# FFN gate and up products as seven-product units, with gated rows kept in DRAM

## The chip, the cores and the metric

The kernel runs on one core of a Trainium2 chip. The metric is the device time of one execution in microseconds. Five engines work beside each other, each in its own order: PE (TensorE, with weight loads as PEld), DVE (VectorE), ACT (ScalarE), POOL (GpSimd) and SP (SyncE), which here issues the DMA transfers.

## The reference

One layer of a decoder for 1024 prompt tokens and 8 sample tokens, 1032 columns together, width 1024, in fp32:

```python
# z = x @ w_in, one projection for all branches and gates
# A: conv4 -> RG-LRU times a gelu gate;  B: sliding-window attention;  C: attention into 256 memory tokens
# mix = (sum of branch @ w_branch, each times sigmoid(gate)) @ w_out
# x <- LN(alpha * x + mix)
# x <- LN(alpha * x + (silu(x @ w_gate) * (x @ w_up)) @ w_down)      D_FF = 2816 = 22 x 128
```

alpha is 2 ** 0.25. The caches of the window, with their new rows, are outputs too.

## The kernel before, in words

Every fp32 operand of a product is a pair, high part and rest (`split`, L69: a cast on ACT, a subtraction on DVE), and a product takes three matmuls (`mm3`, L105 to L107). Tokens lie in the columns: 1032 of them, cut in three chunks of 384, 384 and 264 (`CH`), or in quarters of 258 (`QN`).

Stage 1 (`project`) computes z in 30 units of two row blocks of w_in. A unit is a 2 x 2 block product by seven products instead of eight: both the weights and x enter as sums of their halves. The weight sums are made per unit (`fast_quarter`, L263, then split), three products ahead; a product is two quarters of 258 columns, 12 matmuls each (L279 to L281), 168 matmuls a unit. The sums of x are made once, in `begin`, beside unit 0 (which is computed directly, names u, th, thw) and unit 1. The names there: x and tl are a quarter of x and its rest, ur a raw weight half, us a weight sum, u_3h and u_3l the split of the weights of product 3, za and zb the results. A unit's results are finished by `Finish` (L369, L1182 to L1190).

The branches, the output projection and LN1 (`out_proj`, `layer_norm`) follow. LN1's last step `emit` splits h (hH, L1052, and hL, L1053) and has POOL scale the residual by alpha (L1054).

In the FFN (`ffn`) each of 22 f tiles takes 8 x 3 matmuls per chunk for the gate (fg) and as many for the up product (fu); ft holds silu times up (tanh on ACT, L1068; DVE, L1069 and L1071), and gH, gL its split. Eight, seven and seven f tiles make a part. Behind each of the first two stand its down products (d), added to the residual on DVE (L1095); behind the third those of the last part (dl) with LN2. Two copies of caches to outputs (o_swk, o_swv, 1 MB each) are issued behind the weight loads of f = 2 and f = 4.

The order on each engine is set by a list scheduler from the program's text and its estimates of when operands are ready; `issue_after` holds an instruction behind a given one. Weights pass through rings of six raw buffers of 512 columns, five for high parts and four for rests.

## Time and profile before

| quantity | value |
|---|---|
| median of 3 runs | 2013.3 us (2012.09 to 2013.93) |
| profiled run | 2013.24 us |
| its span, first to last instruction | 2011.5 us |
| mean granted TensorE clock | 0.994 |
| matmuls | 13756 |
| DVE, ACT instructions | 2558, 1921 |
| start of the FFN's first matmul | 1241.61 us |

Busy lines give an engine's busy time, its share of the span and the count of its instructions. In the windows view a row has the stretch, its length, then PE, weight loads, DVE, ACT and POOL as busy us with the count, then the granted clock, the DMA share and GB/s. A timeline row has start, duration, engine, line, operation and tiles, and in brackets the idle time before it with what released it. A group row has its count behind an x, then busy time, mean ns of one, and the idle time before. A DMA row ends with KB of each and the us from issue to landing.

### The profile page before, as it was taken

To read this page: it belongs to the slowest core of one execution; us is meant where nothing else is said; L and a number is where in the kernel's file an instruction comes from. 1 tells how busy PE (TensorE), PEld (TensorE's weight loads), DVE (VectorE), ACT (ScalarE), POOL (GpSimd) and SP (SyncE) were. 2 spreads that over 40 slices of the span, in tenths; PEclk is the share of its full clock that TensorE was granted. 3 is DMA by queue.
4 is the path that set the end of the run, shared out by engine and by line. 5 is a ranking of instruction groups with operands and counts; after the bars stand their busy time and mean duration, and the time that the engine had idled before them with its cause. 6 is when DMAs were issued, how large, how long until landed. Compare 5 with 4: busy or idle time off the path is not lost.

```text
span 2011.5 us, 35413 instructions
## 1 busy us (share of the span) xinstructions
PE 1962.2 (98%) x13756; PEld 1929.8 (96%) x13756; DVE 1197.3 (60%) x2558; ACT 878.9 (44%) x1921; POOL 112.4 (6%) x160
## 2 busy tenths in 40 slices
PE   7999999999999999999999999999999999999997
PEld 7999999999999899989999999999999999999996
DVE  8789778878665555498876658423222332232457
ACT  6556555546564555398763334322111221122324
POOL 0001000000000000021110002100000000000001
PEclk9999999999999999999999999999999999999999
DMA  5454454563233865667435320111111111111102
GB/s 220 151 174 171 165 190 137 176 197 125 76 142 107 294 217 188 160 187 218 121 87 167 124 87 22 63 63 58 48 43 42 53 49 47 53 43 43 57 28 85
DMA packets 140441, 235.44 MB, mean 117 GB/s; under 512 B 17280, under 2 KB 69584, under 8 KB 140240
## 3 DMA queue, kind: packets, MB, share of 16 engines
q1 hardware_dynamic: 140272, 233.17, 35.8%
q8 instruction: 108, 1.77, 0.4%
q14 instruction: 61, 0.50, 0.1%
HBM read 179.95 MB, written 55.23 MB: 117 GB/s over the span
## 4 chain that ended last, share of the span: by engine, by line
PE 70%; ACT 4%; DVE 3%; DMA 3%; issue 1%; SPq 0%; ACTq 0%; POOL 0%; DVEq 0%; POOLq 0%
PE fg L107 4%; PE fg L105 4%; PE fg L106 4%; PE fu L107 4%; PE fu L105 4%; PE fu L106 4%; PE d L105 3%; PE d L107 3%; PE d L106 3%; PE ub L279 2%; PE ub L281 2%; PE ub L280 2%; PE brs L105 2%; PE brs L106 2%; PE brs L107 1%; PE bra L106 1%
## 5 line engine op out<-in xcount | busy, mean ns | idle before, releaser
L105 PE MATMUL fg<-hH,wfg_h 128*128 128x384 f32 (+1 forms) x528 | 169.2, 320 | 5.9 <-ACT wfg_h L71 3.0
L106 PE MATMUL fg<-hL,wfg_h 128*128 128x384 f32 (+1 forms) x528 | 168.4, 319 | 0.4 <-DVE hL L1053 0.4
L107 PE MATMUL fg<-hH,wfg_l 128*128 128x384 f32 (+1 forms) x528 | 168.3, 319 | 0.2
L107 PE MATMUL fu<-hH,wfu_l 128*128 128x384 f32 (+1 forms) x528 | 167.7, 318 | 0.0
L106 PE MATMUL fu<-hL,wfu_h 128*128 128x384 f32 (+1 forms) x528 | 167.6, 317 | 0.0
L105 PE MATMUL fu<-hH,wfu_h 128*128 128x384 f32 (+1 forms) x528 | 167.6, 318 | 0.0
L1071 DVE TENSOR_TENSOR ft<-ft,fu 128x384 f32<-128x384 f32 (+1 forms) x66 | 33.8, 513 | 141.4 <-PE fu L107 141.3
L1069 DVE SCALAR_TENSOR_TENSOR ft<-ft,fg 128x384 f32<-128x384 f32 (+1 forms) x66 | 33.8, 512 | 139.6 <-ACT ft L1068 137.6
L105 PE MATMUL d<-gH,wd_h 128*128 128x384 f32 (+1 forms) x360 | 114.4, 318 | 0.0
L106 PE MATMUL d<-gL,wd_h 128*128 128x384 f32 (+1 forms) x360 | 114.2, 317 | 0.0
L107 PE MATMUL d<-gH,wd_l 128*128 128x384 f32 (+1 forms) x360 | 114.2, 317 | 0.0
L71 ACT CAST gH<-ft 128x384 fp32r<-128x384 f32 (+1 forms) x66 | 31.7, 480 | 183.2 <-DVE ft L1071 183.1
L105 PEld LDWEIGHTS fg<-hH,wfg_h 128*128 128x128 f32 x528 | 99.6, 189 | 7.3 <-ACT wfg_h L71 3.4
L106 PEld LDWEIGHTS fg<-hL,wfg_h 128*128 128x128 f32 x528 | 99.8, 189 | 1.0 <-DVE hL L1053 0.9
L107 PEld LDWEIGHTS fg<-hH,wfg_l 128*128 128x128 f32 x528 | 99.8, 189 | 0.9 <-DVE wfg_l L72 0.9
L107 PEld LDWEIGHTS fu<-hH,wfu_l 128*128 128x128 f32 x528 | 99.2, 188 | 0.0
L105 PEld LDWEIGHTS fu<-hH,wfu_h 128*128 128x128 f32 x528 | 99.2, 188 | 0.0
L106 PEld LDWEIGHTS fu<-hL,wfu_h 128*128 128x128 f32 x528 | 99.2, 188 | 0.0
L1068 ACT ACTIVATE ft<-fg 128x384 f32<-128x384 f32 (+1 forms) x66 | 30.1, 456 | 139.8 <-PE fg L107 139.8
L1095 DVE SCALAR_TENSOR_TENSOR acc<-d,acc 128x384 f32<-128x384 f32 (+1 forms) x48 | 24.8, 516 | 108.4 <-PE d L107 108.4
L565 ACT ACTIVATE bp<-bp,bst 128x257 f32<-128x257 f32 (+1 forms) x128 | 62.8, 493 | 18.1 <-DVE bst L561 18.0
L281 PE MATMUL uc<-th,u_3l 128*128 128x258 f32 x232 | 66.4, 287 | 4.1 <-DVE u_3l L72 4.1
(960 smaller groups left out, 6857.3 us busy)
## 6 DMA issues: line engine op xcount, KB each, us to landing
ur<-win SPq DMA_DIRECT2D x120, 256.0 KB, 2.9
dck<-cmk SPq DMA_DIRECT2D x32, 256.0 KB, 2.9
dcv<-cmvT SPq DMA_DIRECT2D x32, 256.0 KB, 3.5
st<-scr_q SPq DMA_DIRECT2D x32, 256.0 KB, 5.2
scr_g<-za SPq DMA_DIRECT2D x12, 516.0 KB, 3.3
scr_g<-zb SPq DMA_DIRECT2D x12, 516.0 KB, 4.0
x<-xQ SPq DMA_DIRECT2D x8, 516.0 KB, 8.0
scr_a<-ge SPq DMA_DIRECT2D x8, 516.0 KB, 3.0
```

Of the source, the lines that this page charges most:

```text
L71: ins = self.nc.scalar.copy(hi, src).ins
L105: nc.tensor.matmul(ps, sh, mh, start=i == 0, stop=False)
L106: nc.tensor.matmul(ps, sh, ml, start=False, stop=False)
L107: self.last_mm = nc.tensor.matmul(ps, sl, mh, start=False, stop=closes and i == last).ins
L279: mm(sh[:, w], xh, start=opens and k == 0, stop=False)
L280: mm(sh[:, w], xl, start=False, stop=False)
L281: self.last_mm = mm(sl[:, w], xh, start=False, stop=k == 3).ins
L565: nc.scalar.activation(x, x, AF.Exp, bias=st[:, g:g + 1], scale=-1.0, accum_out=st[:, 4 + g:5 + g])
L1068: nc.scalar.activation(t, pg, AF.Tanh, scale=0.5)
L1069: nc.vector.scalar_tensor_tensor(t, t, 1.0, pg, op0=ALU.add, op1=ALU.mult)
L1071: nc.vector.tensor_mul(t, t, pu)
L1095: nc.vector.scalar_tensor_tensor(a, ps, 0.5, a, op0=ALU.mult, op1=ALU.add)
```

## The change

Gate and up of one f tile become one unit of seven products, of the kind of stage 1. The sums of h for it are made by `combine`, a half of the columns of each half of tokens per call, in place in the residual's buffers (16 operations of 1032 columns on DVE over the two calls, 8 casts on ACT); h itself is stored to DRAM from LN1's `emit` and loaded back during units 4 to 11. While the sums are made, f = 0 and 1 are computed as before. The units run in the order 20, 21, 2 to 19. `gated_step` forms silu times up in two halves of tokens, fo1 and fo0, from four partial results (fb, fc, fd banks; fs copies). The halves of 20 and 21 are split and kept; the others, and those of f = 0 and 1, are stored to DRAM and loaded and split again by `load_gated` before the part of the down product that reads them. The down product has four parts: the kept two (dk, in quarters), then 7, 6 and 7 f tiles. Chunks are 388, 386 and 258 columns, which touches the branches and the output projection as well; the residual is held divided by alpha (the multiplication on ACT at L1040 goes, the eps is scaled). The cache copies move to units 14 and 15. In stage 1, product 3 of unit 1 is split right behind product 2, and unit 0's finish and the LRU constants come after products 2 and 4 of unit 1.

```diff
-CH = ((0, 384), (384, 384), (768, 264))
+CH = ((0, 388), (388, 386), (774, 258))
+CW = 388
 NM = 256
 NF = 22
 DEC_AT = (1, 2, 4)
-FPARTS = ((0, 8), (8, 7), (15, 7))
+F_DIRECT = (0, 1)
+F_KEPT = (20, 21)
+F_UNITS = F_KEPT + tuple(range(2, 20))
+F_DOWN = ((0, 7), (14, 6), (7, 7))
+F_CACHE = {8: ("o_swk", "cwk"), 9: ("o_swv", "cwv")}
 NORM_AT = (0, 3)
 LATE = 4
-LAST_CH = ((0, 0, 384), (1, 0, 384), (2, 0, 264))
 BANKS = {"mm": 3, "s": 2, "t": 2, "o": 1}
 HT = T // 2
...
         next_quarter(2)
-        finish.done(*z)
+        next_quarter(3)
...
-        ts = self.begin(finish[0].rows, finish[0], lambda: load(1), lambda i: self.fast_quarter(st[1], i))
+        ts, z0 = self.begin(finish[0].rows, finish[0], lambda: load(1), lambda i: self.fast_quarter(st[1], i))
         with tc.issue_after(self.x_loaded):
             self.load_consts()
             self.load_lru()
-        self.lru_consts()
         todo = [(u, i) for u in range(1, n) for i in range(7)]
         ahead = 3
         for k, (u, i) in enumerate(todo):
             if i == 1 and u + 1 < n:
                 load(u + 1)
-            if k + ahead < len(todo):
+            if 0 < k < len(todo) - ahead:
                 v, j = todo[k + ahead]
                 self.fast_quarter(st[v], j)
             self.fast_step(st[u], i, ts, finish[u])
+            if k == 2:
+                finish[0].done(*z0)
+            if k == 4:
+                self.lru_consts()
             self.pump()
             if i == 6:
                 del st[u]
...
-                nc.scalar.mul(xr, xr, ALPHA)
-                r = self.accs[m][:, t0:t0 + n]
-                nc.vector.scalar_tensor_tensor(r, ps, 0.5, xr, op0=ALU.mult, op1=ALU.add)
+                r = self.M[m][:, t0:t0 + n]
+                nc.vector.scalar_tensor_tensor(r, ps, MIX, xr, op0=ALU.mult, op1=ALU.add)
...
+    def combine(self, p):
+
+        nc = self.nc
+        at = lambda kh, th: self.M4[kh][:, :, HT * th + QN * p:HT * th + QN * (p + 1)]
+        h00, h01, h10, h11 = at(0, 0), at(0, 1), at(1, 0), at(1, 1)
+
+        def keep(j, src, sign=1.0):
+            hi, lo = (a.rearrange("p (k n) -> p k n", k=4) for a in self.S[1][2 * j + p])
+            if sign < 0:
+                self.split_scaled(hi, lo, src, sign)
+            else:
+                self.split(hi, lo, src)
+            return [(hi[:, k, :], lo[:, k, :]) for k in range(4)]
+
+        def direct(kh, th):
+            o = HT * th + QN * p
+            return [tuple(a[:, o:o + QN] for a in self.S[0][4 * kh + k]) for k in range(4)]
+
+        t = {0: direct(0, 0), 3: direct(1, 0), 5: direct(1, 1)}
+        nc.vector.tensor_sub(h11, h11, h01)
+        nc.vector.tensor_sub(h01, h00, h01)
+        t[1] = keep(0, h01)
+        nc.vector.tensor_add(h00, h11, h00)
+        t[2] = keep(1, h00, -1.0)
+        t[4] = keep(2, h11)
+        nc.vector.tensor_sub(h10, h00, h10)
+        t[6] = keep(3, h10)
+        return t
+
+    def gated_step(self, st, i, ts, f):
+
+        nc, ph = self.nc, self.ph
+        small = lambda tag, p: ph.tile([P, QN], F32, tag=tag, name=f"f{tag}{f}_{p}", bufs=2)
+        if i == 1:
+            st["o1"] = ph.tile([P, HT], F32, tag="o1", name=f"fo1{f}", bufs=2)
+        elif i == 3:
+            st["o0"] = ph.tile([P, HT], F32, tag="o0", name=f"fo0{f}", bufs=2)
+        for p in range(2):
+            hp = slice(QN * p, QN * (p + 1))
+            if i in (0, 1, 3):
+                tag, key = {0: ("mm", "b"), 1: ("t", "d"), 3: ("s", "c")}[i]
+                st[key, p] = self.bank(tag, f"f{key}{f}_{p}")[:, :QN]
+            b, c, d = st.get(("b", p)), st.get(("c", p)), st.get(("d", p))
+            self.fast_product(st, i, p, ts, {1: d, 3: c, 5: d}.get(i, b), i in (0, 1, 3))
+            if i in (0, 2):
+                st["s", i, p] = small(f"s{i}", p)
+                nc.scalar.copy(st["s", i, p], b)
+            elif i == 1:
+                nc.scalar.copy(st["o1"][:, hp], d)
+            elif i == 3:
+                s, t = st["s", 0, p], st["o0"][:, hp]
+                nc.vector.tensor_add(s, c, s)
+                nc.scalar.activation(t, s, AF.Tanh, scale=0.5)
+                nc.vector.scalar_tensor_tensor(t, t, 1.0, s, op0=ALU.add, op1=ALU.mult)
+            elif i == 4:
+                o = st["o1"][:, hp]
+                nc.vector.scalar_tensor_tensor(o, b, -1.0, o, op0=ALU.mult, op1=ALU.subtract)
+            elif i == 5:
+                s, t, o = st["s", 2, p], small("t1", p), st["o1"][:, hp]
+                nc.vector.tensor_add(s, d, s)
+                nc.scalar.activation(t, s, AF.Tanh, scale=0.5)
+                nc.vector.scalar_tensor_tensor(t, t, 1.0, s, op0=ALU.add, op1=ALU.mult)
+                nc.vector.tensor_mul(o, t, o)
+            else:
+                o = st["o0"][:, hp]
+                nc.vector.scalar_tensor_tensor(o, o, -1.0, b, op0=ALU.mult, op1=ALU.mult)
+        if i in (5, 6):
+            th = 6 - i
+            o = st[f"o{th}"]
+            if f in F_KEPT:
+                self.split(*(a[:, HT:] for a in self.S[0][2 * F_KEPT.index(f) + th]), o)
+            else:
+                nc.sync.dma_start(self.scr["f"][:, f, HT * th:HT * (th + 1)], o)
+
+    def load_gated(self, f, pair):
+        hi, lo = pair
+        self.nc.sync.dma_start(lo.bitcast(F32), self.scr["f"][:, f, :])
+        self.split(hi, lo, lo.bitcast(F32))
+        return [self.chunk(pair, c) for c in range(3)]
+
...
+        st, ts = {}, []
+
+        def load(f):
+            st[f] = self.fast_load(f"f{f}", io["wgu"][f], io["wgu"][NF + f])
+            st[f]["load"]((0, 0), (0, 1), (1, 0), (1, 1))
+
+        todo = [(f, i) for f in F_UNITS for i in range(7)]
+        with self.phase("ph5a") as self.ph:
+            h = self.out_proj(h)
+            for f in F_DIRECT:
+                for c in range(3):
+                    last = gate_up(f, c, wg, wu)
+                    if (f, c) in ((0, 1), (1, 0)):
+                        with tc.issue_after(self.last_half if f == 0 else last):
+                            ts.append(self.combine(f))
+        g = [[None] * 3 for _ in range(7)]
+        with self.phase("ph5b") as self.ph:
+            self.w1 = self.ph
+            load(F_UNITS[0])
+            for k in range(3):
+                self.fast_quarter(st[todo[k][0]], todo[k][1])
+            for k, (f, i) in enumerate(todo):
+                j = k // 7
+                if i == 1 and j + 1 < len(F_UNITS):
+                    load(F_UNITS[j + 1])
+                    if 4 <= j < 12:
+                        with tc.issue_after(self.last_load):
+                            nc.sync.dma_start(self.M[j - 4], self.scr["h"][:, j - 4, :])
+                    if j in (14, 15):
+                        name, cache = F_CACHE[j - 6]
+                        with tc.issue_after(self.last_load):
+                            nc.sync.dma_start(io[name][:, 0:P - 1, :], io[cache][:, 1:P, :])
+                if k + 3 < len(todo):
+                    v, q = todo[k + 3]
+                    self.fast_quarter(st[v], q)
+                self.gated_step(st[f], i, ts, f)
+                if f == F_UNITS[-1] and i in (2, 4, 6):
+                    for e in {2: range(4), 4: (4, 5), 6: (6,)}[i]:
+                        g[e] = self.load_gated(F_DOWN[0][0] + e, self.S[1][e])
+        with self.phase("ph5c") as self.ph:
+            self.down(g)
+
+    def down(self, g):
+        nc, io = self.nc, self.io
+
+        def add(m, t0, n, ps):
+            a = self.M[m][:, t0:t0 + n]
+            nc.vector.scalar_tensor_tensor(a, ps, MIX, a, op0=ALU.mult, op1=ALU.add)
+
+        cols = lambda f0, nf: slice(f0 * P, (f0 + nf) * P)
+        for m in range(KT):
+            w = self.weights(io["wdn"][m][:, cols(F_KEPT[0], 2)], 2 * P, f"wdk{m}")
+            for th in range(2):
+                for p in range(2):
+                    ps = self.bank(("mm", "s")[p], f"dk{m}_{th}{p}")[:, :QN]
+                    o = HT + QN * p
+                    self.mm3(ps, [(w[j], tuple(a[:, o:o + QN] for a in self.S[0][2 * j + th])) for j in range(2)])
+                    add(m, HT * th + QN * p, QN, ps)
+        f1, n1 = F_DOWN[1]
+        g1 = []
+        for part in range(2):
+            f0, nf = F_DOWN[part]
+            for m in range(KT):
+                w = self.weights(io["wdn"][m][:, cols(f0, nf)], nf * P, f"wd{part}_{m}")
+                if part == 0 and m >= 1 and len(g1) < n1:
+                        g1.append(self.load_gated(f1 + len(g1), self.S[0][(4, 5, 6, 7, 0, 1)[len(g1)]]))
+                if part == 1 and m == 1:
+                    f2, n2 = F_DOWN[2]
+                    with self.tc.issue_after(self.last_load):
+                        g2 = [self.load_gated(f2 + e, self.S[1][e]) for e in range(n2)]
+                act = g1 if part else g
+                for c, (t0, n) in enumerate(CH):
+                    add(m, t0, n, self.mm_tile(w, act, c, f"d{part}_{m}_{c}", nk=nf))
+        f0, nf = F_DOWN[2]
...
```

Three places of the order, without buffer numbers in most names. First DVE in stage 1, unit 1, before, from two rows behind u_2l to u_3l (tl<-x are splits of sums of x; the small rows are constants):

```order
L72 TENSOR_TENSOR tl_0_447<-x_132,th_0_446 128x4x258
L72 TENSOR_TENSOR tl_1_451<-x_136,th_1_450 128x4x258
L204 TENSOR_TENSOR x_122<-x_114,x_122 128x1032
L204 TENSOR_TENSOR x_128<-x_126,x_128 128x1032
L657 TENSOR_SCALAR nsnk<-vec 128x16
L72 TENSOR_TENSOR tl_0_456<-x_122,th_0_455 128x4x258
L659 TENSOR_SCALAR hbg<-vec 128x24
L72 TENSOR_TENSOR tl_1_461<-x_128,th_1_460 128x4x258
L660 TENSOR_SCALAR lruc<-vec 128x8
L661 TENSOR_SCALAR lruc<-vec 128x8
L662 SCALAR_TENSOR_TENSOR lruc<-vec 128x8
L72 TENSOR_TENSOR u_3l<-ur_01_330,u_3h 128x512
```

And with the change:

```order
L80 TENSOR_TENSOR u_2l<-us_2_430,u_2h 128x512
L80 TENSOR_TENSOR u_3l<-ur_01_332,u_3h 128x512
L80 TENSOR_TENSOR tl_1_445<-x_138,th_1_444 128x4x258
L212 TENSOR_TENSOR x_124<-x_116,x_124 128x1032
L212 TENSOR_TENSOR x_130<-x_128,x_130 128x1032
L272 TENSOR_TENSOR us_4_500<-ur_00_330,ur_10_334 128x512
L80 TENSOR_TENSOR tl_0_450<-x_124,th_0_449 128x4x258
L80 TENSOR_TENSOR tl_1_455<-x_130,th_1_454 128x4x258
L80 TENSOR_TENSOR u_4l<-us_4_500,u_4h 128x512
```

u_3l moved ahead of two splits and two sums of x, the finish and the constants; u_4l now stands behind them.

Second, DVE from the end of the second call of combine (acc is the residual's buffer, S1L a rest of a sum of h) to the first splits and weight sums of unit 20 (uf, usf); the rows of before have no counterpart:

```order
L1089 TENSOR_TENSOR acc_8871<-acc_8871,acc_8870 128x4x258
L1090 TENSOR_TENSOR acc_8870<-acc_8870 128x4x258
L80 TENSOR_TENSOR S1L_13923<-acc_8871,S1H_13922 128x1032
L1092 TENSOR_TENSOR acc_8870<-acc_8871,acc_8870 128x4x258
L80 TENSOR_TENSOR S1L_13915<-acc_8870,S1H_13914 128x1032
L1095 TENSOR_TENSOR acc_8871<-acc_8870,acc_8871 128x4x258
L86 SCALAR_TENSOR_TENSOR S1L_13919<-acc_8870,S1H_13918 128x1032
L1161 TENSOR_TENSOR ft_1_16221<-ft_1_16221,fu_1_16224 128x386
L80 TENSOR_TENSOR S1L_13927<-acc_8871,S1H_13926 128x1032
L1159 SCALAR_TENSOR_TENSOR ft_2_16276<-ft_2_16276,fg_2_16251 128x258
L80 TENSOR_TENSOR uf_0l<-urf_00_16310,uf_0h 128x512
L1161 TENSOR_TENSOR ft_2_16276<-ft_2_16276,fu_2_16279 128x258
```

All four sums and four splits of this call stand ahead of the first split of the unit's weights.

Third, ACT before, from f = 4 to the casts for f = 5:

```order
L1068 ACTIVATE ft_0_17033<-fg_0_17008 128x384
L71 CAST gH_0_17062<-ft_0_17033 128x384
L1068 ACTIVATE ft_1_17091<-fg_1_17066 128x384
L71 CAST gH_1_17120<-ft_1_17091 128x384
L1068 ACTIVATE ft_2_17149<-fg_2_17124 128x264
L71 CAST gH_2_17178<-ft_2_17149 128x264
L71 CAST wfg_h<-wfg5r__17182 128x512
L71 CAST wfg_h<-wfg5r__17188 128x512
```

And DVE with the change, where unit 16 ends and 17 begins:

```order
L1129 TENSOR_TENSOR fs_1_20489<-fd_1_20443,fs_1_20489 128x258
L1131 SCALAR_TENSOR_TENSOR ft_1_20593<-ft_1_20593,fs_1_20489 128x258
L1135 SCALAR_TENSOR_TENSOR fo_20495<-fo_20495,fb_0_20384 128x258
L1132 TENSOR_TENSOR fo_20428<-ft_1_20593,fo_20428 128x258
L1135 SCALAR_TENSOR_TENSOR fo_20495<-fo_20495,fb_1_20399 128x258
L80 TENSOR_TENSOR uf_0l<-urf_00_20414,uf_0h 128x512
L272 TENSOR_TENSOR usf_1_20558<-urf_10_20418,urf_11_20420 128x512
L272 TENSOR_TENSOR usf_2_20599<-usf_1_20558,urf_00_20414 128x512
L272 TENSOR_TENSOR usf_4_20674<-urf_00_20414,urf_10_20418 128x512
```

Before, the casts of the next tile's weights stand behind the last gH cast at f = 5; now the first split and the weight sums of unit 17 stand behind the last operation on the fo tile of unit 16.

More of the change, by code (lines that the diff above doesn't have):

```diff
@@ L59, in __init__, with pairs, chunk @@
         self.ctx = ctx
-    def slot(self, kind, c, name, which, n=None):
-        tag = f"{kind}{c}"
-        return self.slots[which].tile([P, n or CH[c][1]], F32R, tag=tag, name=name, bufs=8)
+    def pairs(self, pool, name):
+        return [tuple(pool.tile([P, T], F32R, tag=f"{e}{k}", name=f"{name}{e}{k}", bufs=1) for e in "HL") for k in range(KT)]
+    def chunk(self, pair, c):
+        t0, n = CH[c]
+        return tuple(a[:, t0:t0 + n] for a in pair)
     def bank(self, tag, name):
@@ L628, in product @@
         if step == 2:
-            hi, lo = (self.slot(e, c, f"m{e}{m}_{c}", 0) for e in "HL")
+            hi, lo = self.chunk(self.S[0][m], c)
             self.split(hi, lo, dst)
@@ L899, in resident @@
             k0, k1 = 3 * c, min(3 * c + 3, nk)
-            n = (k1 - k0) * P
-            hi, lo = (self.slot(e, c, f"{name}{e}{c}", which, n) for e in "HL")
+            hi, lo = self.chunk(pair, c)
             for e, raw in enumerate(raws):
@@ L1024, in out_proj @@
         nc, io, ph = self.nc, self.io, self.ph
-        self.accs = [self.acc.tile([P, T], F32, tag="acc", name=f"acc{m}", bufs=8) for m in range(KT)]
         h = [[None] * 3 for _ in range(KT)]
@@ L1141, in build @@
         self.act, self.merged = {}, [[None] * 3 for _ in range(KT)]
-        with pool("acc") as self.acc, pool("slots0", "right") as slots0:
-            self.slots = [slots0]
-            self.M = [self.acc.tile([P, T], F32, tag="acc", name=f"M{m}", bufs=8) for m in range(KT)]
+        with pool("acc") as acc, pool("slots0", "right") as slots0:
+            self.S = [self.pairs(slots0, "S0")]
+            self.M4 = [acc.tile([P, 4, T], F32, tag=f"acc{i}", name=f"acc{i}", bufs=1) for i in range(2)]
+            self.M = [self.M4[m // 4][:, m % 4, :] for m in range(KT)]
             with ExitStack() as gp:
@@ L1163, in build @@
                     gp.close()
[L1164 to L1165 removed]
+                    self.ffn(self.merged)
 class Finish:
```

112 lines of the change are left out of this document (48 added, 64 removed).

## The prediction

> **What bounds the kernel now.** I read the page's busy lines first, then the chain that ended last, then the FFN stretch in the windows view, since that is where the change works.
>
> ```profile
> PE 1962.2 (98%) x13756; PEld 1929.8 (96%) x13756; DVE 1197.3 (60%) x2558; ACT 878.9 (44%) x1921; POOL 112.4 (6%) x160
> PE 70%; ACT 4%; DVE 3%; DMA 3%; issue 1%; SPq 0%; ACTq 0%; POOL 0%; DVEq 0%; POOLq 0%
> 1500.00:1600.00 100.00, 100.00 (x636) 100.00 (x635) 29.01 (x53) 19.45 (x37) 0.00 (x0) 1.00 0.14 43
> 400.00:500.00 100.00, 97.64 (x806) 96.84 (x805) 75.12 (x147) 56.91 (x113) 3.87 (x5) 1.00 0.48 162
> 500.00:600.00 100.00, 100.00 (x824) 100.00 (x823) 67.67 (x109) 59.72 (x107) 3.82 (x5) 1.00 0.31 107
> ```
>
> PE is busy for 98% of the span and carries 70% of the chain. In the FFN (1500 to 1600) it never stops, at full clock (the column of 1.00), with DVE at 29% and DMA at 0.14. The other two windows are the projection stage, which already runs seven-product units: PE is full from 500 to 600 with DVE at 68%, and loses 2.4% from 400 to 500 with DVE at 75%. So the FFN is bound by matmul time, and the sum is first a count of matmuls times their spacing.
>
> **Prices.** Busy time of a matmul overlaps its neighbour, so I take start-to-start times. The rows are the first matmul of two consecutive f tiles and of two consecutive units, and matmuls of the down product.
>
> ```profile
> 1541.48 0.34 PE L105 MATMUL fg<-hH,wfg_h 128*128 128x384 f32 x1
> 1563.97 0.34 PE L105 MATMUL fg<-hH,wfg_h 128*128 128x384 f32 x1
> 617.31 0.28 PE L279 MATMUL ub<-th,u_0h 128*128 128x258 f32 x1
> 637.48 0.28 PE L279 MATMUL ub<-th,u_0h 128*128 128x258 f32 x1
> 1503.79 0.33 PE L105 MATMUL d<-gH,wd_h 128*128 128x384 f32 x1
> 1504.31 0.33 PE L105 MATMUL d<-gH,wd_h 128*128 128x384 f32 x1
> 1504.83 0.28 PE L105 MATMUL d<-gH,wd_h 128*128 128x264 f32 x1
> 1505.19 0.29 PE L105 MATMUL d<-gH,wd_h 128*128 128x264 f32 x1
> ```
>
> One f tile: 22.49 us. One unit without other work: 20.17 us for 168 matmuls, 120.1 ns each. Three 384-column matmuls take 0.52 us, 173 ns each; 264 columns take about 121.7 ns (an f tile is 96 of the one and 48 of the other). The slope, 0.43 ns a column, makes 388 columns 175.0 and 386 columns 174.2.
>
> **Gate and up.** Before, 22 x 22.49 = 494.8 us. After, two tiles stay direct with the new widths: 48 x (175.0 + 174.2 + 120.1) = 22.53 each, 45.1 together; twenty units cost 20 x 20.17 = 403.4. Difference **-46.3**. A rule speaks against this term: the Trainium skill, page "TensorE: Matmul & The Clock Gate", section "Back-to-back issue gap", gives about 81 ns a matmul at 128 columns and 131 at 512 in a real stream of weight loads and matmuls. Interpolated, an estimate, that is 98 ns at 258 and 114 at 384: a unit of 168 small matmuls would take 16.5 us and an f tile 15.8, and the twenty units would lose about 15 us. The trace disagrees at both widths (120.1 and 173), so the sum goes by the rows.
>
> **Down and the rest of PE.** Before, 15 gated tiles x 8 outputs = 120 weight tiles, three matmuls on each of three chunks. After, 104 of them in two parts (13 x 8) at 3 x 469.3 ns instead of 3 x 468.3, and two kept tiles as quarters: 8 x 2 x 4 x 3 = 192 matmuls of 258. That is 146.4 + 23.1 against 168.6: **+0.9**. The last part (168 triples) and the 768 triples of branches and output projection pay 1 ns a triple for the new widths: **+1.0**.
>
> **What hides the new DVE and ACT work.** A unit has seven weight splits and four weight sums of 512 columns and 16 operations of 258 on DVE.
>
> ```profile
> L263 DVE TENSOR_TENSOR us<-us,ur 128x512 f32<-128x512 f32 x58 | 39.8, 686 | 0.9
> L72 DVE TENSOR_TENSOR u_1l<-us,u_1h 128x512 fp32r<-128x512 f32 x29 | 20.5, 709 | 0.0
> L308 DVE SCALAR_TENSOR_TENSOR zb<-ub,p5s 128x258 f32<-128x258 f32 x58 | 24.3, 420 | 15.8 <-PE ub L281 15.8
> L71 ACT CAST u_0h<-ur 128x512 fp32r<-128x512 f32 x29 | 18.1, 623 | 17.6 <-PE ub L280 14.3 <-DMA scr_a<-ge 1.0 <-DMA dcpb<-dcpd 0.9
> L304 ACT COPY p1s<-ub 128x258 f32<-128x258 f32 x58 | 20.9, 372 | 6.9 <-PE ub L281 6.9
> L1068 ACT ACTIVATE ft<-fg 128x264 f32<-128x264 f32 x22 | 8.5, 384 | 4.3 <-PE fg L107 4.3
> ur<-win SPq DMA_DIRECT2D x120, 256.0 KB, 2.9
> scr_g<-za SPq DMA_DIRECT2D x12, 516.0 KB, 3.3
> gts<-scr_g SPq DMA_DIRECT2D x8, 516.0 KB, 3.8
> ```
>
> DVE: 11 x 0.69 + 16 x 0.42 = 14.3 us; ACT: 7 x 0.62 + 6 x 0.37 + 4 x 0.38 = 8.1; both under PE's 20.17, with splits made three products (8.6 us) ahead. The DMA of a unit is 1 MB of weights (as an f tile had) and two stores of half a 516 KB tile, each bounded by 3.3 us; loads of a unit are issued a unit ahead. The reloads of gated tiles (3.8 us each) go before the parts that read them. I take 0 for twenty steady units; the bounds are 0 and the excess of rival B.
>
> **The start.** In the rows below, PE stops in unit 1 because its fourth split is late on DVE, and runs at half clock afterwards.
>
> ```profile
> 40.00:50.00 10.00, 5.89 (x37) 5.69 (x36) 10.00 (x28) 5.00 (x9) 0.00 (x0) 0.83 0.33 115
> 60.00:70.00 10.00, 10.00 (x85) 10.00 (x84) 10.00 (x25) 4.81 (x11) 0.00 (x0) 1.00 0.46 158
> 80.00:90.00 10.00, 10.00 (x83) 10.00 (x82) 4.16 (x7) 5.54 (x13) 0.00 (x0) 1.00 0.40 143
> 32.56 0.28 PE L279 MATMUL ub<-th,u_0h 128*128 128x258 f32 x1
> 46.18 0.39 PE L281 MATMUL uc<-th,u_3l 128*128 128x258 f32 x1 [4.11 <-DVE u_3l L72]
> 58.84 0.28 PE L279 MATMUL ub<-th,u_0h 128*128 128x258 f32 x1
> 36.28 0.68 DVE L72 TENSOR_TENSOR u_2l<-us,u_2h 128x512 fp32r<-128x512 f32 x1
> 38.02 2.55 DVE L72 TENSOR_TENSOR tl<-x,th 128x1032 fp32r<-128x1032 f32 x2
> 45.44 0.69 DVE L72 TENSOR_TENSOR u_3l<-ur,u_3h 128x512 fp32r<-128x512 f32 x1
> ```
>
> Unit 1 lasts 58.84 - 32.56 = 26.28 us against 20.17. The order now puts u_3l right behind u_2l, so it ends near 37.6, ahead of PE's need at 41.7. Next late are u_4l, behind three wide splits and two wide sums of x (1.15 us each at their spacing) plus one weight sum, until about 45.5 where PE wants it at 44.3 (a wait of about 1.0 behind the first matmuls), and the first split of unit 2 (0.6). Unit 1 then ends near 54.6: 4.2 less. But DVE stays full until 70, with the displaced work (hi_xq rows of 1.2 us, small constants) behind it, so part may be paid back before the slack of 80 to 90. I take **-4.0**, bounds -6 and 0.
>
> **Stalls that go, stalls that come.** At f = 3 and f = 5 PE waits for the weight casts that the ACT order holds behind a gH cast.
>
> ```profile
> 1310.64 0.28 PE L107 MATMUL fu<-hH,wfu_l 128*128 128x264 f32 x1
> 1312.40 0.44 PE L105 MATMUL fg<-hH,wfg_h 128*128 128x384 f32 x1 [1.49 <-ACT wfg_h L71]
> 1321.21 0.33 PE L105 MATMUL fg<-hH,wfg_h 128*128 128x384 f32 x1
> 1357.74 0.28 PE L107 MATMUL fu<-hH,wfu_l 128*128 128x264 f32 x1
> 1369.89 0.33 PE L105 MATMUL fg<-hH,wfg_h 128*128 128x384 f32 x1
> L204 DVE TENSOR_TENSOR x<-x,x 128x1032 f32<-128x1032 f32 x8 | 9.6, 1223 | 0.0
> 1264.78 1.03 DVE L1053 SCALAR_TENSOR_TENSOR hL<-acc,vec,hH 128x264 fp32r<-128x264 f32 x2
> 1266.83 0.34 PE L107 MATMUL fg<-hH,wfg_l 128*128 128x384 f32 x1
> ```
>
> From the last fu of one tile to the second chunk of the next should take 0.12 + 8.32 us; it took 10.57 and 12.15 (the second with half clock behind its gap). Both go: **-5.8**. The cache copies beside them move to units 14 and 15, and the order shows unit 17's first splits behind the last operation of unit 16's fo tile: 2 x 0.34 of DVE after PE's last product and a split, **+0.9**.
>
> The larger new wait stands before the first unit, 20. The two calls of combine put 16 operations of 1032 columns (1.15 us each at their spacing, 18.4) on DVE, with four weight splits, seven gate operations (5.3) and waits for casts (about 1.6) between them, all ahead of uf20_0l. They begin at about 1265.8, where the last hL ends, so uf20_0l starts near 1291.1; PE, through with f = 1 at 1266.8 + 22.5 = 1289.3, then waits about 2.4 us for its low half, and about 1.3 more since the cast of the second quarter stands on ACT behind copies of the first product: **+3.7**, bounds 0 (combine overlaps better) and 8. The gap of 1.49 us at f = 3 left the clock alone and the one at f = 5 was followed by about 1.6 us of loss at half clock; half of that, **+0.8**. By the rule of the same page of the Trainium skill, section "What's actually happening" (half clock after an idle window of about 3.4 us), the gap at f = 5 should have cost none, so the trace disagrees and the row decides; by the rule this term is 0. Bank handovers at the load of gated tiles and between down parts: **+0.6**, bounds 0 and 3.
>
> **The sum.** -46.3 + 0.9 + 1.0 - 4.0 - 5.8 + 0.9 + 3.7 + 0.8 + 0.6 = **-48.2**. The profiled run took 2013.24 us (span 2011.5 and 1.74 around it), 0.06 under the median of 2013.3; so 1965.0 by the run and **1965** against the median.
>
> **Rivals.** *B, units wait on their helpers.* Each unit sends four pieces through PE, DVE, ACT's tanh and DVE again, which the projection's units don't; on DVE the next unit's splits queue behind such a round trip. The projection's window of 400 to 500 lost 2.36 us of 100, which is 0.5 us a unit; with once to twice that the twenty units cost +10 to +20, 1975 to 1985. For it: DVE at 14.3 of 20.2, with waits in order. Against: the lead of three products, and the window of 500 to 600, which lost nothing. *C, slower than before:* the same round trips in full. If each of the four made DVE stand for over 2.1 us, DVE's unit would be 14.3 + 8.4 = 22.7 us, and past 20.17 + 48.2 / 20 = 22.6 the kernel is slower: 2.2 us each make 23.1 and 2024. The tanh takes 0.38 and a cast or two ahead of it 0.62, so about 1 us is the most I see. *D, the side gains fail:* the start pays all back (+4), combine costs 8 (+4) and handovers 3 (+2): 1975. It lies in the range of A. *E, less than the sum takes:* combine hidden and the start at -6: 1958. *F, a matmul's price hardly depends on its width:* at the f tile's mean of 156.2 ns for each (22.49 / 144) a unit's 168 would take 26.2 us and the twenty +121: 2086. The units' 20.17 us leaves this next to no room. It is the direction of the spacing rule cited above.
>
> **Chances.** A with D and E (1955 to 1975) 0.74; B 0.18; C 0.05, of which 0.02 lies within 0.2% of before (about what a measurement of this kernel can tell from no change); F 0.01; below 1955, 0.02. The range takes in the nearer part of B: 1955 to 1983. Faster 0.94, same 0.02, slower 0.04.
>
> **What would show it.** Right: unit starts 20.2 us apart for f = 2 to 19; u_3l gone from PE's waits; no cast wait at a direct tile; one gap of 2 to 5 us before the first fb product. Wrong, B or C: PE waits on uf splits or fs copies in every unit, DVE above 85% there. If loads lag, PE's waits end on urf or on gated tiles.

## The result: faster, by a little less than forecast

The change takes 1969.99 us (median of 4 runs, 1969.5 to 1971.11) against 2012.69 before (4 runs): a ratio of 0.9781, 95% interval 0.9767 to 0.9796. The forecast was 1965 with a range of 1955 to 1983. The profiled run took 1969.6 us, 43.6 less than the profiled run of before, where the sum had 48.2.

The page of the change, busy lines and chain:

```profile
span 1967.8 us, 37173 instructions
PE 1921.1 (98%) x14284; PEld 1888.8 (96%) x14284; DVE 1350.4 (69%) x2872; ACT 951.4 (48%) x2071; POOL 118.7 (6%) x160
PE 84%; DVE 5%; ACT 4%; DMA 4%; issue 1%; SPq 0%; POOL 0%; ACTq 0%; DVEq 0%; POOLq 0%
```

PE has 528 matmuls more and 41 us less busy time; it still bounds the kernel. The timeline rows of PE at which stages begin, before (first branch product, first product of the FFN, f = 2, first product of the last down part):

```profile
662.42 0.69 PE L105 MATMUL bra<-baH,wba_h 128*128 128x384 f32 x1 [4.61 <-ACT baH L71]
1237.85 0.33 PE L105 MATMUL fu<-hH,wfu_h 128*128 128x384 f32 x1
1288.27 0.34 PE L105 MATMUL fg<-hH,wfg_h 128*128 128x384 f32 x1
1912.53 0.34 PE L105 MATMUL dl<-gH,wdl0H 128*128 128x384 f32 x1
```

The 1241.61 us that stands in the table of before as the start of the FFN is its first gate matmul; its first matmul is this one of the up product, at 1237.85. And with the change (the same, with the starts of units 20, 21, 2 and 19, and of dk):

```profile
657.07 0.69 PE L113 MATMUL bra<-S0H,wba_h 128*128 128x388 f32 x1 [5.19 <-ACT S0H L79]
1234.21 0.34 PE L113 MATMUL fu<-S0H,wfu_h 128*128 128x388 f32 x1
1287.04 0.28 PE L287 MATMUL fb<-S0H,uf_0h 128*128 128x258 f32 x1
1311.21 0.28 PE L287 MATMUL fb<-S0H,uf_0h 128*128 128x258 f32 x1
1331.40 0.28 PE L287 MATMUL fb<-S0H,uf_0h 128*128 128x258 f32 x1
1675.74 0.28 PE L287 MATMUL fb<-S0H,uf_0h 128*128 128x258 f32 x1
1695.93 0.28 PE L113 MATMUL dk<-S0H,wdk_h 128*128 128x258 f32 x1
1868.89 0.34 PE L113 MATMUL dl<-S1H,S0H 128*128 128x388 f32 x1
```

Unit 21 lasts 1331.40 - 1311.21 = 20.19 us, and so do sixteen more; unit 20 lasts 24.17. The differences of these rows, beside the terms of the prediction (d before is 168.7 us, two stretches of the timeline; its two extra stalls are counted with the tiles):

| stretch | before, us | change, us | difference | predicted |
|---|---|---|---|---|
| start to first branch product | 662.4 | 657.1 | -5.4 | -4.0 |
| branches, output projection | 575.4 | 577.1 | +1.7 | +0.8 |
| f = 0 and 1, direct | 50.4 | 52.8 | +2.4 | +0.1 |
| the other 20 tiles | 455.6 | 408.9 | -46.7 | -46.8 |
| down product without the last part | 168.7 | 173.0 | +4.3 | +1.5 |
| last part, LN2, end of span | 98.9 | 98.9 | 0.0 | +0.2 |
| sum | 2011.5 | 1967.8 | -43.7 | -48.2 |

What PE waits for in and around the FFN with the change (us in all, times, longest):

```profile
PE bra L113 <- ACT S0H L79: 5.2, 1, 5.2
PE fg L113 <- ACT S0H L1059: 3.0, 1, 3.0
PE fb L289 <- DVE uf_0l L80: 2.3, 2, 1.6
PE fg L113 <- DVE acc L1049: 1.6, 1, 1.6
PE dk L113 <- DVE fo L1135: 1.3, 1, 1.3
PE fd L287 <- ACT uf_1h L79: 1.0, 1, 1.0
PE fb L287 <- DVE ft L1161: 0.6, 1, 0.6
```

The waits for u_3l and for the weight casts wfg_h, which the prediction shows for the kernel before, are gone. The three fb and fd waits belong to unit 20, with one of 0.8 us of uf_0l at unit 17. New in size is fg's wait for S0H, the high part of h in the third chunk. Windows around it (PE, PEld, DVE, ACT, POOL busy; clock; DMA share; GB/s), and one inside the units:

```profile
1234.00:1257.00 23.00, 18.52 (x106) 17.65 (x104) 17.38 (x38) 9.60 (x19) 4.75 (x5) 1.00 0.24 87
1257.00:1263.00 6.00, 5.86 (x34) 5.75 (x35) 6.00 (x13) 3.72 (x9) 4.41 (x6) 0.72 0.04 14
1400.00:1500.00 100.00, 100.00 (x835) 100.00 (x834) 61.71 (x125) 39.22 (x84) 0.00 (x0) 1.00 0.33 106
```

PE is full in the units with DVE at 62%; after the 3.0 us wait it ran at half clock for 3.4 us (1258.5 to 1262.0).

### The profile page after: what moved, and what is told of

Same layout as the page of the kernel before. It is cut to its first block, busy times and chain, and to the rows that moved or that the text cites. A ratio compares the mean times of both kernels' runs of the same rounds, so it can differ in the third digit from the quotient of the medians.

```text
span 1967.8 us, 37173 instructions
## 1 busy us (share of the span) xinstructions
PE 1921.1 (98%) x14284; PEld 1888.8 (96%) x14284; DVE 1350.4 (69%) x2872; ACT 951.4 (48%) x2071; POOL 118.7 (6%) x160
## 3 DMA queue, kind: packets, MB, share of 16 engines
q8 instruction: 112, 1.84, 0.4%
## 4 chain that ended last, share of the span: by engine, by line
PE 84%; DVE 5%; ACT 4%; DMA 4%; issue 1%; SPq 0%; POOL 0%; ACTq 0%; DVEq 0%; POOLq 0%
PE ub L289 5%; PE ub L287 5%; PE ub L288 5%; PE fb L289 4%; PE fb L287 4%; PE fb L288 4%; PE d L114 3%; PE d L115 3%; PE ud L289 3%; PE d L113 2%; PE ud L288 2%; PE ud L287 2%; PE fd L287 2%; PE fd L289 2%; PE fd L288 2%; PE brs L114 2%
## 5 line engine op out<-in xcount | busy, mean ns | idle before, releaser
L289 PE MATMUL ub<-th,u_0l 128*128 128x258 f32 x232 | 66.1, 285 | 1.6 <-DVE u_0l L80 1.6
L287 PE MATMUL ub<-th,u_0h 128*128 128x258 f32 x232 | 65.9, 284 | 1.4 <-ACT zb L1331 1.4
L289 PE MATMUL ub<-th,u_6l 128*128 128x258 f32 x232 | 66.0, 284 | 0.0
L289 PE MATMUL ud<-th,u_1l 128*128 128x258 f32 x232 | 66.0, 284 | 0.0
L287 PE MATMUL ub<-th,u_6h 128*128 128x258 f32 x232 | 66.0, 284 | 0.0
L287 PE MATMUL ub<-th,u_4h 128*128 128x258 f32 x232 | 65.9, 284 | 0.0
L287 PE MATMUL ub<-th,u_2h 128*128 128x258 f32 x232 | 65.8, 284 | 0.0
L289 PE MATMUL ub<-th,u_4l 128*128 128x258 f32 x232 | 65.8, 283 | 0.0
L289 PE MATMUL ub<-th,u_2l 128*128 128x258 f32 x232 | 65.8, 283 | 0.0
L289 PE MATMUL ud<-th,u_5l 128*128 128x258 f32 x232 | 65.8, 283 | 0.0
```

Of the source, the lines that this page charges most:

```text
L287: mm(sh[:, w], xh, start=opens and k == 0, stop=False)
L289: self.last_mm = mm(sl[:, w], xh, start=False, stop=k == 3).ins
```

## The experiments

The later runs had before at 2014.3 to 2015.2 us, so whole times are compared as ratios to it; the change stands at 0.9781. Places are compared in the traces.

**e1, widths alone in the kernel before.**

```diff
-CH = ((0, 384), (384, 384), (768, 264))
+CH = ((0, 388), (388, 386), (774, 258))
-LAST_CH = ((0, 0, 384), (1, 0, 384), (2, 0, 264))
+LAST_CH = ((0, 0, 388), (1, 0, 386), (2, 0, 258))
-            t = ph.tile([P, 384], F32, tag="gt", name=f"ft{f}_{c}", bufs=3)[:, :n]
+            t = ph.tile([P, 388], F32, tag="gt", name=f"ft{f}_{c}", bufs=2)[:, :n]
```

> The kernel before with the chunks of the change (388, 386, 258; one gate buffer fewer, for room). Theory 1 (width alone sets the spacing, and 384 columns are cheaper than their neighbours): in the trace of the change a triple of the three widths takes 473.5 ns against 468.5, so the 2352 triples here cost +11 to +12 us: ratio 1.0055 to 1.006. Theory 2 (the prediction's slope of 0.43 ns a column): +1.0 ns a triple, +2.4 us. Theory 3 (the slower spacing comes from reading chunks as slices of one long row, which this kernel doesn't do): about +2.

Measured: 1.0066 (1.0051 to 1.0081), 13 us slower. Matmuls of 386 columns in its down product, six apart:

```profile
1500.01 0.34 PE L105 MATMUL d<-gH,wd_h 128*128 128x386 f32 x1
1501.07 0.34 PE L105 MATMUL d<-gH,wd_h 128*128 128x386 f32 x1
```

That is 176.7 ns each, where 384 columns took 173.3. Over all its down products (d) the means are 177.1 at 388, 177.4 at 386 and 120.4 at 258 (before: 173.5 at 384, 121.7 at 264). Width alone does it, in buffers of their own, and between 384 and 386 it is a step and no slope: theory 1. The gate buffer fewer is not in it, since d does not use these buffers.

**e2, the old widths in the change.**

```diff
-CH = ((0, 388), (388, 386), (774, 258))
-CW = 388
+CH = ((0, 384), (384, 384), (768, 264))
+CW = 384
```

> The change with the old chunks (384, 384, 264), still slices of one long row. Theory 1: 1344 triples at 4.9 ns less, -6.6 us; against it, the first call of combine now waits for the third chunk's LN1 (its columns end at 774), so that the first split of unit 20 comes later by about 3 us; net -2 to -5 against the change, 1965 to 1968. Theory 2: -1.3 + 3, 1972. Theory 3 (slices): no spacing gain, 1973.

Measured: 0.9780 (0.9763 to 0.9796), the change's time, where -2 to -5 us was expected. Branches and output projection are 1.8 us shorter, but unit 20 lasts 29.23 in place of 24.17 (its starts):

```profile
1284.48 0.28 PE L287 MATMUL fb<-S0H,uf_0h 128*128 128x258 f32 x1
1313.71 0.28 PE L287 MATMUL fb<-S0H,uf_0h 128*128 128x258 f32 x1
```

In e2 the first operation of combine starts at 1267.72 in place of 1264.15, behind a store of h to DRAM, so the later boundary does hold combine back. But only 1.4 us of the 5.1 is a longer wait (2.0 us in place of 0.6 before the first product of unit 20). The rest is half clock, from 1288.3 to 1298.6, here in e2 and in the change:

```profile
1290.00:1293.00 3.00, 3.00 (x16) 3.00 (x16) 1.17 (x2) 0.38 (x1) 0.00 (x0) 0.50 0.33 101
1290.00:1293.00 3.00, 2.68 (x20) 2.47 (x20) 2.26 (x5) 0.57 (x2) 0.00 (x0) 1.00 0.13 44
```

So the two effects of theory 1 were seen and cancelled, the second mostly through the clock. Theory 3 (slices) is not shown: 384 columns took 174.4 ns in d here against 173.5 before, but before's output projection and last down part, which read buffers of their own, took 174.3 too.

**e3, the reordered first sums alone in the kernel before.**

```diff
         next_quarter(2)
-        finish.done(*z)
+        next_quarter(3)
...
-        self.lru_consts()
...
-            if k + ahead < len(todo):
+            if 0 < k < len(todo) - ahead:
...
             self.fast_step(st[u], i, ts, finish[u])
+            if k == 2:
+                finish[0].done(*z0)
+            if k == 4:
+                self.lru_consts()
```

> The kernel before with the reordered first sums alone. The prediction's term: -4.0 (bounds -6 and 0). The trace of the change had the branch products start at 657.07 against 662.4, so theory 1 is -5 to -6, ratio 0.997. Rival: the time is paid back behind DVE, which stays full until 80 us, 0 to -2.

Measured: 0.9962 (0.9949 to 0.9976), -5 to -10 us; span 2005.6 against 2011.5. The first branch product:

```profile
658.26 0.69 PE L105 MATMUL bra<-baH,wba_h 128*128 128x384 f32 x1 [5.42 <-ACT baH L71]
```

It comes 4.2 us earlier with the wait there 0.8 longer, so the projection gained 5. The gain does not all lie at the start. Counted by matmuls, the 501st of the kernel (in the third unit) starts 2.7 us earlier than before and the 1251st 1.8 us earlier, so about 1 us is paid back; the gain grows to 5.0 only between the 3001st and the 3501st (380 to 440 us). There the trace of e4, which has the old start, also gains 1.5. Another 1.6 is in the gate products: the gap at f = 5 was there as before, but no half clock followed it.

**e4, the cache copies moved in the kernel before.**

```diff
-                if f in (2, 4):
-                    name, cache = (("o_swk", "cwk"), ("o_swv", "cwv"))[f // 2 - 1]
+                if f in (9, 11):
+                    name, cache = (("o_swk", "cwk"), ("o_swv", "cwv"))[(f - 9) // 2]
```

> The kernel before with the two cache copies behind the weight loads of f = 9 and 11 in place of 2 and 4. Theory 1 (the copies put the next weight casts late in ACT's order): the waits at f = 3 and 5 are gone, and the same wait of 1.5 us stands at f = 10 and 12, net -2 to +2, depending on half clock. Rival (the waits belong to the f tiles behind LN1, not to the copies): waits stay at f = 3 and 5 and the time is the same within 1 us.

Measured: 0.9996 (0.9986 to 1.0006). Waits for weight casts in the gate product:

```profile
PE fg L105 <- ACT wfg_h L71: 1.5, 1, 1.5
```

One is left of two (3.0 us before), at 1608.2, a tile behind the second copy; those of f = 3 and 5 are gone. So the copies make the wait, through the order of casts (the casts for f = 12 stand on ACT behind the last gH cast of the tile before); the rival falls. The whole time is the same within its interval.

**e5, four units turned back into direct tiles.**

```diff
-F_DIRECT = (0, 1)
+F_DIRECT = (0, 1, 2, 3, 4, 5)
-F_UNITS = F_KEPT + tuple(range(2, 20))
+F_UNITS = F_KEPT + tuple(range(6, 20))
-                    if j in (14, 15):
-                        name, cache = F_CACHE[j - 6]
+                    if j in (11, 12):
+                        name, cache = F_CACHE[j - 3]
```

> The change with f = 0 to 5 computed directly and sixteen units (6 to 19 and the kept two). Theory 1: each of four units turned back costs 48 x 473.5 ns = 22.73 in place of 20.19: +10.2 us against the change; by the prediction's prices (22.53 and 20.17) +9.4. A price that hardly depends on width (rival F): units dearer than tiles, so faster than the change. Rival B (units wait on helpers): under +8.

Measured: 0.9834 (0.9818 to 0.9851), 10.7 us above the change. First up product, first unit, first dk product:

```profile
1237.02 0.34 PE L113 MATMUL fu<-S0H,wfu_h 128*128 128x388 f32 x1
1382.06 0.28 PE L287 MATMUL fb<-S0H,uf_0h 128*128 128x258 f32 x1
1707.49 0.28 PE L113 MATMUL dk<-S0H,wdk_h 128*128 128x258 f32 x1
```

Six direct tiles took 145.0 us, two took 52.8 in the change: 23.05 for each more. The units took 325.4 in place of 408.9, 83.5 less: four units at 20.19 are 80.8, and the rest is the wait of unit 20, gone where the sums of h had been ready long before. A direct tile costs 2.9 us more than a unit. Rivals B (under +8) and F (faster) fall here.

**e6 and e7, more DVE work in each unit.** Both add sums whose result is not used, 16 and 32 a unit (4 and 8 at each of four places):

```diff
                 nc.scalar.copy(st["s", i, p], b)
+                x = ph.tile([P, QN], F32, tag="x", name=f"fx{f}_{i}{p}", bufs=1)
+                for _ in range(4):
+                    nc.vector.tensor_add(x, st["s", i, p], st["s", i, p])
```

> The change with sixteen extra DVE sums of 258 columns in each unit (results not used), 0.34 to 0.42 us each, 5.4 to 6.7 a unit; DVE was busy 60 to 64% in the units, so it comes to 18 to 19.7 of 20.19. Theory 1 (DVE's work is covered by PE): 0 to +2 us. Theory 2 (rival B or C: the margin is thin since DVE waits in order for ACT and PE): PE waits in each unit, +20 or more.

> The change with thirty-two such sums in each unit, 10.9 to 13.4 us: DVE needs 23.3 to 26 of 20.19. Both theories: DVE is the bound; twenty units at that length, +60 to +115 us. It gives the price of a unit when DVE decides, and so the margin.

Windows inside the units, e6:

```profile
1400.00:1500.00 100.00, 100.00 (x834) 100.00 (x834) 88.62 (x204) 39.50 (x85) 0.00 (x0) 1.00 0.33 107
```

and e7:

```profile
1400.00:1500.00 100.00, 92.22 (x715) 89.67 (x714) 96.33 (x241) 34.52 (x72) 0.00 (x0) 0.97 0.30 96
```

e6: with DVE at 89% PE is still full, and the units last 20.19. From the first up product to the last down part the stretch is 2.2 us longer than the change's, 1.3 of it in dk: about theory 1's upper end, and far from the +20 of theory 2. The whole time was 0.9810 (0.9796 to 0.9825), 5.8 us more, with an interval of about 3 us either way; its trace shows 3.9 more, of which the other 1.7 lie ahead of the FFN, where the edit changes nothing. e7 took 2048.8 us in its one run, about 79 above the change and inside the forecast; PE waits for DVE and gets through 14% fewer matmuls. So the 5.4 us a unit that e6 added (88.62 - 61.71 of 100 us) cost the steady units nothing, and rival C's point lies beyond them.

**e8, stored twice.**

```diff
                 nc.sync.dma_start(self.scr["f"][:, f, HT * th:HT * (th + 1)], o)
+                nc.sync.dma_start(self.scr["f2"][:, f, HT * th:HT * (th + 1)], o)
```

> The change with every half of a gated row that goes to DRAM stored twice (a second scratch, never read). Theory 1 (stores are off the path): 0, within 1 us. Theory 2 (stores in SP's queue hold the next unit's weight loads): up to 3.3 us for each unit whose loads are late, +10 or more.

Measured: 0.9789 (0.9775 to 0.9804). Units last 20.19, and the FFN to the last down part 635.0 us against 634.7 (1868.89 - 1234.21). The stores are off the path.

**e9, another middle way of widths.**

```diff
-CH = ((0, 388), (388, 386), (774, 258))
-CW = 388
+CH = ((0, 384), (384, 390), (774, 258))
+CW = 390
```

> The change with chunks of 384, 390 and 258: the first at the cheap width, the boundary at 774 kept, so that combine waits for nothing new. Theory 1 (spacing jumps just above 384 columns and is nearly flat from 386 to 390): 384 at 174.4, 390 at 177 to 178.5, 258 at 119 to 120: a triple 1 to 3 ns cheaper than 473.8, 1344 triples: -1.5 to -4 us, and a shorter wait for the third chunk of LN1 (3.0 to about 1.2 to 2): -2 to -6 in all. Theory 2 (a slope by columns): 0.

Measured: 0.9781 (0.9764 to 0.9798). In d, 384 columns took 174.3 ns, 390 took 177.7 and 258 took 118.6: 470.6 a triple against 474.1, theory 1 again, 1.0 us in d. The wait of LN1's third chunk stayed at 3.0. Whole times don't tell it from the change.

**e10, three operations of combine later.**

```diff
         t[2] = keep(1, h00, -1.0)
-        t[4] = keep(2, h11)
-        nc.vector.tensor_sub(h10, h00, h10)
-        t[6] = keep(3, h10)
+
+        def rest():
+            t[4] = keep(2, h11)
+            nc.vector.tensor_sub(h10, h00, h10)
+            t[6] = keep(3, h10)
+
+        if p == 0:
+            rest()
+        else:
+            self.rest = rest
         return t
...
+            with tc.issue_after(self.last_sub):
+                self.rest()
             for k, (f, i) in enumerate(todo):
```

> The change with the last three operations of combine's second call (the split of sum 4, the sum and the split of 6; 3 x 1.15 us on DVE) issued behind the first three weight splits of unit 20, which need neither. Theory 1 (unit 20 waits only for the DVE rows ahead of its first split): the three waits of 0.6, 1.6 and 1.0 us before and in its first products go, -2.5 to -3.6, and unit 20 lasts about 20.5 in place of 24.17. Rival (it waits for the weight loads or for buffers freed by f = 1): unit 20 stays near 24, time the same.

The starts of units 20 and 21:

```profile
1289.07 0.28 PE L287 MATMUL fb<-S0H,uf_0h 128*128 128x258 f32 x1
1310.56 0.28 PE L287 MATMUL fb<-S0H,uf_0h 128*128 128x258 f32 x1
```

Unit 20 lasts 21.49, 2.7 less; what is left is mainly the wait of 1.0 for uf_1h. So it waited for the DVE rows ahead of its first split, as the prediction had it. The ratio is 0.9774 (0.9760 to 0.9789), not told from the change's by whole times.

**e11, both, with other banks for dk and the copies in the third down part.**

```diff
-                    ps = self.bank(("mm", "s")[p], f"dk{m}_{th}{p}")[:, :QN]
+                    ps = self.bank(("t", "s")[p], f"dk{m}_{th}{p}")[:, :QN]
...
+                if part == 1 and m in (4, 5):
+                    name, cache = F_CACHE[m + 4]
+                    with self.tc.issue_after(self.last_load):
+                        nc.sync.dma_start(io[name][:, 0:P - 1, :], io[cache][:, 1:P, :])
```

> Both edits together, with the banks of the kept down products (dk) taken from the two tags that are free by then in place of the last unit's, and the cache copies issued behind the weights of outputs 4 and 5 of the third down part. Theory 1: e9 and e10 add, the dk wait of 1.3 us goes (the bank of the last unit's product is what it waits for) and unit 17's 0.9 (the second copy is what delays its loads): -7 to -12 against the change. Rival for dk (it waits for the gated rows or the weights): 1.3 stays; rival for unit 17: 0.9 stays in the units.

Measured: 0.9778 (0.9759 to 0.9797). Waits of PE:

```profile
PE dk L113 <- DVE acc L1219: 1.7, 2, 1.1
PE d L115 <- DVE wd_l L80: 1.5, 2, 0.8
```

The waits of unit 17 are gone, and the copies made two of 0.8 where they went. The dk wait changed its name and hardly its size: PE gets twelve matmuls further and then waits for its own first additions, which stand on DVE behind the last unit's operations. So the last unit's banks alone are not its cause. By whole times e11 is not told from the change, and the forecast of -7 to -12 fell.

**e12, gated tiles reloaded later.** The chunks of e9, the edit of e10, and:

```diff
-                if f == F_UNITS[-1] and i in (2, 4, 6):
-                    for e in {2: range(4), 4: (4, 5), 6: (6,)}[i]:
+                if f == F_UNITS[-1] and i == 2:
+                    for e in (0, 1):
...
+            if 1 <= m <= 5:
+                with self.tc.issue_after(self.last_load):
+                    g[m + 1] = self.load_gated(F_DOWN[0][0] + m + 1, self.S[1][m + 1])
```

> The change with three edits: the chunks of e9, combine's late operations of e10, and the reloads of five gated tiles spread over the kept down products, so that two instead of four of their 1.15 us splits stand on DVE among the last unit's operations. Theory 1 (the first dk product waits for DVE's backlog: with other banks in e11 it waited as long, for the first addition): the dk wait of 1.3 to 1.5 us goes or halves; with e10's 2.3 and e9's 1.5 in the FFN's stretch, -4 to -6 there against the change's 720.6 us from the first up product to PE's last matmul. Rival (it waits for the banks of the last unit as such): 1.3 stays, -3 to -4.

Measured: median 1968.55, 0.9775 (0.9757 to 0.9793). First up product, first product of the last down part, and the wait:

```profile
1235.12 0.34 PE L113 MATMUL fu<-S0H,wfu_h 128*128 128x384 f32 x1
1865.68 0.34 PE L113 MATMUL dl<-S1H,S0H 128*128 128x384 f32 x1
PE dk L113 <- DVE fo L1142: 1.4, 1, 1.4
```

This stretch takes 630.6 us, 4.1 less than in the change; to PE's last matmul, the stretch of the forecast, it is 715.9 against 720.6, 4.7 less and inside -4 to -6. The reason given there is not shown: e9 and e10 alone were 1.5 and 2.3 shorter in that stretch, 3.9 together, and the dk wait stays. Nor did the edit do what it was meant to: five splits of reloaded tiles still run on DVE ahead of the last unit's last operations, where the change has six. So e12 leaves the question of the backlog open. In both traces ACT waits with the cast of such a tile until its reload has landed, and a tanh of the last unit stands in order behind it (the change, then e12):

```profile
1693.61 1.06 ACT L79 CAST S1H<-S1L 128x1032 fp32r<-128x1032 f32 x1 [1.95 <-DMA S1L<-scr_f]
1694.57 0.42 ACT L1130 ACTIVATE ft<-fs 128x258 f32<-128x258 f32 x1
1692.65 1.06 ACT L79 CAST S1H<-S1L 128x1032 fp32r<-128x1032 f32 x1 [3.24 <-DMA S1L<-scr_f]
1693.62 0.42 ACT L1137 ACTIVATE ft<-fs 128x258 f32<-128x258 f32 x1
```

e12 has the shortest trace (span 1964.6), but by whole times it is not told from the change.

## Why the prediction was right, and where its sum was off

**Gate and up, the units.** Right to 0.1 us together with the stalls: units of 20.19 against the 20.17 taken from the projection. 528 more matmuls took less time, and turning units back cost time (e5), so rival F falls. With it falls, for this kernel, the spacing rule of the Trainium skill, page "TensorE: Matmul & The Clock Gate", section "Back-to-back issue gap". (Its interpolation, an estimate, gives 15.7 us for an f tile and not the 15.8 of the prediction; the sign stays.)

**Hidden DVE, ACT and DMA work.** Right: e6 raised DVE's work, e8 doubled the stores, and the units kept their length. ACT's work was not raised in any run; it stood at 39%. DVE measured 12.5 us a unit (61.71 of 100 us), under the 14.3 of the sum: its rows of 0.42 us start 0.34 apart, so durations overlap.

**Where the 4.5 us are.** The sum fell 4.5 us short of its -48.2. Against their terms the down products took 2.8 more, the direct tiles 2.3 and the branches 0.9; the start gave 1.4 more than forecast, and the rest is 0.1 or 0.2.

**Widths: the term that was mis-sized.** The prediction put 388 and 386 columns on a slope of 0.43 ns a column and took +1.0 ns a triple. In d a triple took 474.1 ns against 468.6 (147.9 us for 312, 168.7 for 360), +5.5; e1 shows the width as the cause. Over 1344 triples of the change (768, 312, 168 and 96) that is an estimate of about +7 in place of +1.4. It makes half of the miss in the down products (1.7 us in d in place of 0.3) and about 0.4 of the 2.3 in the direct tiles. The branches grew by 1.7 us only, where the widths alone would make 3.8; what offset the rest was not traced, and the same stretch took 2.3 us longer in e4 than before, with no edit there.

**The start.** Right in its cause, partly lucky in its size. The wait for u_3l and the half clock behind it are gone, and the 501st matmul starts 3.2 us earlier than before; at the 1251st 2.3 are left, so a part was paid back as the prediction allowed. The -5.4 at the first branch product takes another 3.1 that came at 380 to 440 us, where the prediction had nothing; e3 has the same there (3.3), e4 half of it, and it was not traced.

**The copies.** Right in cause (e4). They carried the wait along: 1.2 us at units 16 and 17 (predicted 0.9), two of 0.8 in e11.

**Before unit 20.** Waits of 0.6, 1.6 and 1.0 us, 4.0 us over a steady unit, against 3.7 predicted; e5 and e10 take most of it away with the rows ahead of it on DVE. The +0.8 for half clock did not come there, as the window rule of the Trainium skill cited in the prediction had it; but half clock did come behind a wait of 3.0 us, shorter than the 3.4 of that rule, and there the measurement decides.

**The direct tiles.** That wait of 3.0 us, fg's for the third chunk of LN1, is a place where the prediction had nothing. It was 3.0 in the change and in e9 and 3.3 in e1, and 1.2 to 1.3 before and in e2. The traces show the operation: with a third chunk of 258 columns the order puts LN1's reciprocal behind the gate operation ft of the second chunk, for which DVE stands 2.2 us until PE has finished; with 264 it stands ahead. First the change, then before:

```profile
1253.78 0.56 DVE L1161 TENSOR_TENSOR ft<-ft,fu 128x386 f32<-128x386 f32 x1 [2.24 <-PE fu L115]
1254.26 1.76 DVE L956 RECIPROCAL n1rs<-n1rs 128x258 f32<-128x258 f32 x1
1255.43 1.80 DVE L947 RECIPROCAL n1rs<-n1rs 128x264 f32<-128x264 f32 x1 [1.24 <-ACT n1rs L944]
1257.19 0.55 DVE L1071 TENSOR_TENSOR ft<-ft,fu 128x384 f32<-128x384 f32 x1
```

The reciprocal's input was ready at 1252.87, so it starts 1.4 us late and PE in the end waits for itself. No run changed this order alone. With the half clock behind it this makes about 1.9 of the 2.4 us that the direct tiles cost more.

**Handover to dk.** 1.9 us in two waits against 0.6. Other banks (e11) did not remove it, and e12 hardly thinned the splits in DVE's way, so it did not test them. The last unit's chain of sum, tanh and product ends on DVE about 3.4 us after PE's last product. The rows shown with e12 name a suspect: the tanh starts about 1.2 us after its input is there, since the cast ahead of it waits for a reload from DRAM. No run moved it alone, so the cause stays open.

## What to carry to other kernels

Price a matmul at the exact width the change gives it: two columns more can cost more than a slope through distant widths says. When a PE-bound stage gets fewer columns to move, count first what of the new work stands in order ahead of the first product; the steady stage hid some 5.4 us a unit of further DVE work, while three rows (3.5 us) moved behind the first splits of the first unit won 2.7 us there. An operation that delays the scheduler's casts carried its wait along in three runs (e4, e11 and the change). After an edit of sizes, read the order again: here 6 columns fewer swapped two DVE operations and made PE wait 1.8 us longer.

## What the runs showed of the hardware beyond that

- Matmul spacing has a step between 384 and 386 columns: in the down products it was 173.5 ns at 384 (before), 177.4 at 386 and 177.1 at 388 (e1, buffers of their own). With the operand a slice of a row of 1032 it was 174.4 at 384 (e2), 176.6 at 386 and 178.4 at 388 (the change), and 177.7 at 390 (e9).
- Half clock does not follow the length of a gap but the idle time in fixed stretches of time. In each trace the stretches at half clock inside the kernel last 3.41 us, or twice or three times that, and start whole multiples of 3.41 us apart (before: 46.43, 660.83 and 1360.56, 180 and 205 of them). Cut on this grid, the 14 traces show no half clock behind a stretch of 3.41 us at full clock in which PE stood idle for less than 1.58 us, and always half clock behind one with more than 1.84 us; between the two both occur. Before, at f = 3, at f = 5 and right behind f = 5, and e3 at f = 5:

```profile
1309.36:1312.78 3.42, 1.94 (x15) 1.65 (x14) 1.26 (x3) 1.36 (x4) 0.00 (x0) 1.00 0.00 0
1357.15:1360.56 3.41, 1.82 (x12) 1.29 (x11) 1.94 (x4) 2.04 (x5) 0.00 (x0) 1.00 0.00 0
1360.56:1363.98 3.42, 3.42 (x13) 3.42 (x12) 1.42 (x3) 0.98 (x2) 0.00 (x0) 0.50 0.67 243
1351.56:1354.98 3.42, 1.98 (x17) 1.77 (x15) 0.88 (x3) 0.94 (x3) 0.00 (x0) 1.00 0.00 0
```

PE was idle for 1.48, 1.59 and 1.44 us in the first, second and last of these; half clock came behind the second alone. So a gap of 1.5 us is at the edge, and where it falls on the grid decides. The three waits of unit 20 fall into three stretches (1.31, 0.83 and 0.98 us idle) and cost no clock, the 3.0 us wait leaves 2.01 us in one, and in e2 two waits of unit 20 fall together (2.91).
